# Output-projection pieces as separate jobs in the TensorE order table, and the last layer's norm on VectorE in another order

## Chip, cores and metric

One NeuronCore of one Trainium2 chip runs the whole program in one launch. Its engines work in parallel, each on its own in-order queue: TensorE (PE; matmuls, with PEld for its weight loads), VectorE (DVE), ScalarE (ACT), GpSimd (POOL), and SyncE (SP), which only starts DMAs here. The metric is the device time in microseconds (us), and less is better. Times are medians of several runs. One further execution was profiled, and all rows below are of that one.

## Reference

The kernel computes a trunk of four decoder layers on one sequence of 512 tokens with 1024 features. Layers 0 and 3 use latent attention (`mla`), layer 1 sliding-window attention (`swa`), layer 2 forgetting attention (`fox`). What matters here is the end of a layer:

```python
return (o * jax.nn.silu(gate)) @ w_out          # end of each branch
...
x = _layernorm(DEEPNORM_ALPHA * x + y, ln_g[i], ln_b[i])

def _layernorm(x, g, b):
    xf = x.astype(jnp.float32)
    mu = jnp.mean(xf, axis=-1, keepdims=True)
    var = jnp.mean(jnp.square(xf - mu), axis=-1, keepdims=True)
    y = (xf - mu) * lax.rsqrt(var + LN_EPS) * g.astype(jnp.float32) + b.astype(jnp.float32)
    return y.astype(x.dtype)
```

`o` holds 16 heads of width 64 side by side, so the output projection contracts over 1024 values: eight pairs of heads, 128 values each.

## The kernel before

**Tiling.** The 512 tokens are four blocks of 128 (`tb` 0 to 3). Matrix products are made of values split into a high and a low part, so a product of one 128-deep slice takes three matmuls: high x high, low x high and high x low (`tokproj_steps`; the order of the three is high-high, low-high, high-low for the left operand and the weight). A matmul writes up to 128 x 512 values into a PSUM bank. The pools of banks are `ps_p` (three banks, "pp" in the profile), `ps_s` and `ps_t` (two each) and `ps_o` (one, "oo").

**A layer.** Projections make the queries, keys, values and gates, pair by pair of heads. For each head there are logits (`s` steps; "ss"), a softmax on VectorE, ScalarE and GpSimd, transposes of the probabilities on TensorE (`t` steps; "ptt", evacuated by ScalarE at L500 and VectorE at L325 into "PT"), and the product with the values (`o` steps, `attn_pv`; "oo"). After the odd head of a pair, `attn_pv` evacuates the bank (ScalarE L543, VectorE L544), multiplies by the gate (GpSimd L551, VectorE for the last pair) and writes the pair's high part (ScalarE L552) and low part (L325) into the tile `oT`. These are the left operands of the output projection, so a matmul of the projection for pair k can run only when pair k is there.

**The output projection** gives 4 token blocks x 2 halves of 512 columns, each a sum over 8 pairs: 24 matmuls for one (half, block). `out_part` makes them in pieces: half 0 of blocks 0, 1 and 2 for the pairs 0 to 5 (18 matmuls each), then pair 6 of the same three (3 each), then half 1 of blocks 0, 1, 2 and half 0 of block 3 for the pairs 0 to 6 (21 each). Pair 7 is added at the end (`ends`, letter `k`), and half 1 of block 3 (`last_mm`, letter `m`) is made there as a whole. `out_part` is one generator, which gives these 147 matmuls in this fixed order.

**The order of TensorE** within a layer is written out by hand in the strings of `ORDER`. A word is a letter and a count: `s`, `t` and `o` are the steps named above; `f`, `g` and `h` take a step (in this part one matmul) of the first, second or third job of a list of unfinished jobs. The jobs are the projections of `STREAM`, and last of all the output projection as one job with 1000 steps. Where fewer jobs are left than the letter asks for, the index is cut to the last one:

```python
job = jobs[min("fgh".index(w[0]), len(jobs) - 1)] if w[0] in "fgh" else [0, runs[w[0]]]
```

So where the output projection alone is left, `f`, `g` and `h` all mean its next matmul. `tail` then adds the last two heads with fixed numbers of projection steps between them, and `finish` the end of the layer. During `ORDER` and `tail` only TensorE's order is as written; the other engines' orders are laid out when the program is built. In `finish` only VectorE's order is as written.

**The end of a layer** is the string of `FINISH` for that layer. Each word puts operations on VectorE and hands out the work for other engines that belongs to it:

- `f`, `k`, `m`: matmuls of the projection, as above.
- `r`, `h`, `i` (`out_res`, L586): residual plus projection for both halves, half 0 or half 1 of a block, in place in the tile `r`, with the row sums.
- `s` (`ln_stats`, L612 and L614): the negative mean on VectorE, then the squares of the whole block on ScalarE, added up.
- `t` (`ln_rstd`, L619 and L620): variance plus epsilon on VectorE, then the power -0.5 on GpSimd.
- `a` and `b` (`ln_apply`, L634): (r + negative mean) x gain, then x 1/sigma + offset; each is two passes of 128 x 512 on VectorE. `b` starts the DMA that stores the block. In the last layer block 3 goes to another tile (`y`) and is stored by halves.
- `z` (`ln_apply_side`, L645 to L651; last layer, block 0 alone): the same norm on ScalarE (one pass) and GpSimd (four passes).
- `x`: transposes of the block for the next layer (not in the last).

Of the kernel before, what the change touches and what calls it, by code (L numbers as in the profile page):

```python
# [12 lines left out]
F32 = mybir.dt.float32  # L13
F32R = mybir.dt.float32r
BF16 = mybir.dt.bfloat16
AF = mybir.ActivationFunctionType
ALU = mybir.AluOpType
# [3 lines left out]
D = 1024  # L21
S = 512
NT = S // 128
# [15 lines left out]
FINISH = (  # L39
# [4 lines left out]
)  # L44
PRO = ((2, 1, 2, 2), (2, 1, 19, 0))
TAIL = ((3, 4, 6, 6), (2, 10, 2, 5), (9, 0, 4, 9), (6, 3, 7, 2))
# [154 lines left out]
class Net:  # L201
# [355 lines left out]
    def out_part(self, layer, st):  # L557

        st["acc"] = {}
        st["done"] = 0  # L560
        st["stat"] = self.p_st.tile([128, NT, 4], F32, tag="stat", name=self.nm("stat"))
        self.load_residual(layer, st)
        parts = [(0, tb, range(6)) for tb in range(3)] + [(0, tb, [6]) for tb in range(3)]
        parts += [(half, tb, range(7)) for half, tb in ((1, 0), (1, 1), (1, 2), (0, 3))]
        for half, tb, ks in parts:
            for _ in self.out_mm(layer, st, half, tb, list(ks), False):
                st["done"] += 1 if self.fine else 3
                yield

    def out_mm(self, layer, st, half, tb, ks, stop):  # L570
        if (half, tb) not in st["acc"]:
            if (half, tb) in ((1, 0), (1, 1)):
                st["acc"][(half, tb)] = self.ps_s.tile([128, 512], F32, tag="ss", name=self.nm("po"))
            elif (half, tb) in ((1, 2), (0, 3)):
                st["acc"][(half, tb)] = self.ps_t.tile([128, 512], F32, tag="pt", name=self.nm("po"))
            else:
                st["acc"][(half, tb)] = self.bank()
        out = st["acc"][(half, tb)][:]
        oT = st["oT"]
        return self.tokproj_steps(out, lambda k: (self.W(layer, "O", half, k // 2), (k % 2) * 512), 512,  # L580
                                  lambda k, a, b: oT[k // 2][:, k % 2, a, b * 128:(b + 1) * 128], tb, ks, ks[0] == 0, stop, 3)
# [26 lines left out]
    def ln_stats(self, st, tb):  # L608
# [4 lines left out]
        jk = self.p_g.tile([128, D], BF16, tag="g", name=self.nm("jk"))  # L613
        nc.scalar.activation(jk[:], st["r"][tb][:], AF.Square, bias=s[:, 2:3], scale=1.0, accum_out=s[:, 3:4])  # L614

    def ln_rstd(self, st, tb):
        nc = self.nc
        s = st["stat"][:, tb, 3:4]
        nc.vector.tensor_scalar(s, s, 1.0 / D, LN_EPS, op0=ALU.mult, op1=ALU.add)  # L619
        nc.gpsimd.tensor_tensor(s, s, self.half[:, 0:1], op=ALU.pow)  # L620

    def ln_apply(self, layer, st, tb, part):
# [14 lines left out]
                nc.sync.dma_start(dst[:, cols], r[:, cols])  # L637
        if part and not halves:
            nc.sync.dma_start(dst, r[:])

    def ln_apply_side(self, st, tb):

        nc = self.nc
        r, s = st["r"][tb], st["stat"][:, tb]
        nc.vector.tensor_tensor(s[:, 2:3], s[:, 2:3], s[:, 3:4], op=ALU.mult)  # L645
        nc.scalar.activation(r[:], r[:], AF.Identity, bias=s[:, 2:3], scale=s[:, 3:4])
        for part, op in ((0, ALU.mult), (1, ALU.add)):
            for c in range(2):
                v = r[:, c * 512:(c + 1) * 512]
                nc.gpsimd.tensor_tensor(v, v, st["gb"][2 * part + c][:], op=op)  # L650
        nc.sync.dma_start(self.t["out"][tb * 128:(tb + 1) * 128, :], r[:])  # L651


    def run_heads(self, layer, st, make, pre=None, npre=0):

        kind = layer % 3
        st["P"], st["PT"], st["oT"] = {}, {}, []
        st["np"] = 3 if kind == 0 else 2
        self.heads = 0

        def size(n):
            return {"K": 6, "Q": 9, "R": 9}.get(n, 24) if kind == 0 else 96 if n == "V" else 24

        def logits():
            for h in range(H - 1):
                if h == 13 and kind == 0:
                    self.cq_done(layer)
                for i, f in enumerate(st["s_fn"](h, st)):
                    for j, _ in enumerate(f()):
                        if i == NT - 1 and j == st["np"] - 1:  # L670
                            self.head_done()
                        yield

        jobs = [[npre, pre]] if npre else []
        jobs += [[size(n), make[n](a)] for n, a in STREAM[kind]]
        st["order"] = self.out_part(layer, st)
        jobs.append([1000, st["order"]])
        runs = {"s": logits(), "t": chain.from_iterable(f() for h in range(H - 2) for f in st["t_fn"](h, st)),
                "o": chain.from_iterable(self.attn_pv(h, st) for h in range(H - 2))}
        self.fine = True  # L680
        with self.tc.manual_schedule(engines={mybir.EngineType.PE}):
            for w in ORDER[layer].split():
                for _ in range(int(w[1:])):
                    job = jobs[min("fgh".index(w[0]), len(jobs) - 1)] if w[0] in "fgh" else [0, runs[w[0]]]
                    next(job[1])
                    job[0] -= 1
                    while jobs[0][0] == 0:
                        jobs.pop(0)
            assert len(jobs) == 1 and all(next(r, None) is None for r in runs.values())
            self.tail(layer, st)  # L690

    def tail(self, layer, st):
# [12 lines left out]
    def finish(self, layer, st):  # L705
        nc = self.nc
        self.load_gb(layer, st)
        self.layer = layer + 1
        if layer < DEPTH - 1:
            self.new_xT()  # L710

        def mm(half, tb, ks=(7,)):
            self.run(self.out_mm(layer, st, half, tb, list(ks), True))

        def res(tb, half):
            self.out_res(layer, st, half, tb, st["acc"][(half, tb)][:])

        S0, S1 = lambda tb: self.ln_stats(st, tb), lambda tb: self.ln_rstd(st, tb)
        A = lambda tb, i: self.ln_apply(layer, st, tb, i)

        def X(tb):
            self.x_transposes(st["r"][tb], tb, (self.ps_s, "ss") if tb % 2 == 0 else (self.ps_t, "pt"))

        def ends(tb):
            assert st["done"] >= (84, 105, 126, 147)[tb]
            mm(0, tb)
            if tb < 3:
                mm(1, tb)

        last_mm = self.out_mm(layer, st, 1, 3, list(range(8)), True)  # L730
        todo = {"f": lambda n: self.run(islice(st["order"], n)), "k": ends, "m": lambda n: self.run(islice(last_mm, n)),
                "r": lambda t: (res(t, 0), res(t, 1)), "h": lambda t: res(t, 0), "i": lambda t: res(t, 1), "s": S0, "t": S1,
                "a": lambda t: A(t, 0), "b": lambda t: A(t, 1), "z": lambda t: self.ln_apply_side(st, t), "x": X}
        with self.tc.manual_schedule(engines={mybir.EngineType.DVE}):
            for w in FINISH[layer].split():
                todo[w[0]](int(w[1:]))
# [404 lines left out]
```

## Time and profile before

| | |
|---|---|
| median of 3 runs | 1026.9 us (1026.78 to 1029.99) |
| the profiled execution's own time | 1026.01 us |
| its span, first to last instruction | 1024.2 us |
| mean granted TensorE clock | 0.986 of full |
| DMA over the span | 116.79 MB, mean 114 GB/s |

How to read the rows: a timeline row has the start and the duration in us, the engine, the line of the program, the operation, output and inputs, the shape, and how many instructions were merged into it; in brackets stands the idle time of the engine before it and the instruction that ended it. L322 is the helper that issues every matmul, so matmuls are told apart by their tiles: "pp" or "po" with `oT` is the output projection. A wait row has the total, the number and the longest. A window row has the stretch, its length, the busy time of each engine with its number of instructions, the granted clock (1.00 is full), the share of DMA time and GB/s.

### The profile page before, as it was taken

The page shows a single profiled execution, that of the slowest core. Times are in us where ns is not written, and L with a number is a line of the kernel's source. Part 1 is how long each engine was busy: PE and PEld are TensorE (multiplying, and loading weights), DVE is VectorE, ACT ScalarE, POOL GpSimd, SP SyncE. Part 2 cuts the span into 40 slices and gives each one's busy share as a digit, 9 for nine tenths or more (in the row PEclk, how much of TensorE's full clock was granted, in tenths as well). Part 3 has the DMA queues.
Part 4 walks back from the last instruction along what each step waited for, and adds up shares of the span by engine and source line. Part 5 has one row for each costly group of instructions (what it writes and reads, how often), then busy time and mean ns, then how long its engine had stood idle before and what let it go on. Part 6 is the DMA issues. An engine that isn't in the chain of part 4 may idle for free.

```text
span 1024.2 us, 16213 instructions
## 1 busy us (share of the span) xinstructions
PE 985.8 (96%) x5512; PEld 856.9 (84%) x5512; DVE 598.3 (58%) x1501; ACT 620.8 (61%) x1354; POOL 510.7 (50%) x572
## 2 busy tenths in 40 slices
PE   8999999999999999899999999997999999999995
PEld 7979888877988888688888888985779888888784
DVE  2467666935546667528325644664547466667827
ACT  4378888843357777523446766663533478888722
POOL 5746655335156663432556666543254647664213
PEclk9999999999999999899999999998999999999998
DMA  6353332634342213223434323353224354334322
GB/s 225 119 157 92 98 106 66 205 111 146 133 143 84 83 63 124 91 94 128 133 120 141 105 88 120 91 144 120 84 84 146 97 145 127 85 94 124 103 62 83
DMA packets 37795, 116.79 MB, mean 114 GB/s; under 512 B 5440, under 2 KB 5696, under 8 KB 37456
## 3 DMA queue, kind: packets, MB, share of 16 engines
q1 hardware_dynamic: 37712, 115.75, 36.5%
q8 instruction: 44, 0.72, 0.3%
q14 instruction: 39, 0.32, 0.1%
HBM read 92.62 MB, written 8.42 MB: 99 GB/s over the span
## 4 chain that ended last, share of the span: by engine, by line
PE 47%; DVE 3%; issue 2%; POOL 1%; ACT 1%; DMA 1%; DVEq 0%; POOLq 0%; SPq 0%; ACTq 0%
PE pp L322 31%; PE ss L322 4%; PE po L322 4%; PE oo L322 3%; PE ptt L514 3%; DMA wr<-in_w 1%; PE pxt L389 1%; POOL r L650 1%; DVE w L310 1%; DVE r L634 0%; POOL P L462 0%; DVE PT L325 0%; ACT P L451 0%; DVE wo L310 0%; DVE r L586 0%
## 5 line engine op out<-in xcount | busy, mean ns | idle before, releaser
L322 PE MATMUL pp<-xT,w 128*128 128x512 f32 (+1 forms) x1440 | 352.4, 387 | 0.0
L310 POOL TENSOR_TENSOR w<-wr,w 128x512 fp32r<-128x512 f32 (+1 forms) x202 | 242.2, 1224 | 193.0 <-ACT w L306 127.2
L322 PEld LDWEIGHTS pp<-xT,w 128*128 128x128 f32 x1440 | 256.1, 188 | 44.2
L462 POOL TENSOR_TENSOR P<-P,rs 128x256 f32<-128x256 f32 (+2 forms) x192 | 113.0, 616 | 136.8 <-DVE rs L457 131.3
L306 ACT CAST w<-wr 128x1024 fp32r<-128x1024 f32 (+5 forms) x121 | 116.1, 964 | 87.4 <-PE pp L322 43.5
L451 ACT ACTIVATE P<-P,m 128x256 f32<-128x256 f32 (+3 forms) x256 | 137.8, 539 | 45.9 <-DVE m L1069 17.0
L325 DVE TENSOR_TENSOR PT<-ptt,PT 128x384 fp32r<-128x384 f32 (+1 forms) x176 | 104.0, 600 | 52.6 <-ACT PT L500 51.3
L500 ACT CAST PT<-ptt 128x384 fp32r<-128x384 f32 (+1 forms) x176 | 88.3, 515 | 47.6 <-PE ptt L514 34.6
L322 PE MATMUL pp<-w,xT 128*128 128x256 f32 (+2 forms) x768 | 112.7, 300 | 2.9 <-ACT xT L393 2.5
L322 PEld LDWEIGHTS pp<-w,xT 128*128 128x128 f32 x768 | 105.8, 191 | 4.6 <-ACT xT L393 3.1
L322 PE MATMUL oo<-PT,v 128*128 128x256 f32 (+3 forms) x512 | 106.6, 313 | 2.3 <-DVE o L544 1.6
L322 PEld LDWEIGHTS oo<-PT,v 128*128 128x128 f32 x512 | 83.5, 189 | 14.0 <-DVE o L544 2.6
L322 PE MATMUL pp<-w,oT 128*128 128x512 f32 x288 | 82.5, 422 | 10.9 <-ACT oT L552 7.5
L322 PE MATMUL ss<-kt,q 128*128 128x128 f32 (+3 forms) x384 | 81.8, 328 | 2.2 <-ACT kt L838 1.6
L322 PE MATMUL pp<-cT,w 128*128 128x512 f32 x312 | 81.6, 397 | 0.0
L885 DVE CUSTOM_DVE_ANT_0 P<-ss,mask 128x128 f32<-128x128 f32 (+3 forms) x128 | 61.1, 484 | 32.4 <-PE ss L322 24.7
L514 PE MATMUL ptt<-ident,P 128*128 128x128 f32 x480 | 78.5, 275 | 1.5 <-DVE PT L325 0.8
L322 PEld LDWEIGHTS pp<-w,oT 128*128 128x128 f32 x288 | 56.0, 202 | 23.4 <-ACT oT L552 8.1
L322 PE MATMUL po<-wo,oT 128*128 128x512 f32 x288 | 71.5, 396 | 0.0
L322 PEld LDWEIGHTS ss<-kt,q 128*128 128x128 f32 x384 | 60.7, 189 | 8.8 <-ACT kt L838 2.2
L514 PEld LDWEIGHTS ptt<-ident,P 128*128 128x128 f32 x480 | 57.1, 140 | 11.8 <-PE ss L322 2.1
L544 DVE TENSOR_TENSOR o<-oo,o 64x512 f32<-64x512 f32 x64 | 43.9, 686 | 37.4 <-ACT o L543 36.7
(120 smaller groups left out, 1425.9 us busy)
## 6 DMA issues: line engine op xcount, KB each, us to landing
wr<-in_w SPq DMA_DIRECT2D x106, 512.0 KB, 3.5
q<-rq SPq DMA_DIRECT2D x64, 128.0 KB, 2.4
xd<-r SPq DMA_DIRECT2D x12, 512.0 KB, 2.9
r<-xd SPq DMA_DIRECT2D x12, 512.0 KB, 3.4
wr<-in_w SPq DMA_DIRECT2D x16, 336.0 KB, 3.4
kd<-kd SPq DMA_DIRECT2D x20, 256.0 KB, 3.2
tq<-in_cs SPq DMA_DIRECT2D x8, 512.0 KB, 4.0
cb<-cd SPq DMA_DIRECT2D x16, 256.0 KB, 3.9
```

What stands on the lines that cost most here:

```text
L306: nc.scalar.copy(w[0][:, :c], r[:, :c])
L310: eng.tensor_tensor(w[1][:, a:b], r[:, a:b], w[0][:, a:b].bitcast(F32), op=ALU.subtract)
L322: self.nc.tensor.matmul(out, l, r, start=start, stop=stop)
L325: (eng or self.nc.vector).tensor_tensor(out, src, hi.bitcast(F32), op=ALU.subtract)
L389: nc.tensor.transpose(v, xt[:, c:c + 128], self.ident[:])
L451: nc.scalar.activation(v, v, AF.Exp, bias=m[:, c:c + 1], scale=-1.0, accum_out=sums[:, c:c + 1])
L462: nc.gpsimd.tensor_tensor(v, v, rs[:, c:c + 1].to_broadcast([128, v.shape[1]]), op=ALU.mult)
L500: nc.scalar.copy(pt[:, 0, :n], ps[:, :n])
L514: nc.tensor.transpose(ps[:, c:c + 128], Ps[qb][:, kb * 128:(kb + 1) * 128], self.ident[:])
L544: nc.vector.tensor_tensor(o[a, :], o_ps[a, :], o[a, :], op=ALU.add)
L650: nc.gpsimd.tensor_tensor(v, v, st["gb"][2 * part + c][:], op=op)
L885: nc.vector.tensor_tensor_reduce(out=P[:, :n], in0=ps[:, :n], in1=self.mask[:, S - n:], scale=1.0, scalar=3e38, op0=ALU.add, op1=ALU.min, ...
```

## The change

It has three parts. First, `out_part` no longer is one generator but returns a list of ten jobs, one for each piece, with its number of matmuls; they are appended to the list of jobs, and the index is not cut. So `g` and `h` now mean the next and the one after the next piece once only pieces are left. What is unfinished is chained for `tail`. The strings of `ORDER` are unchanged. Second, the last layer's string of `FINISH` has another order, and block 0's norm is made by `a0` and `b0` on VectorE; `ln_apply_side` is gone. Third, block 3's squares are made by halves (`p3`: the first half about its own mean, after `h3`; `q3`: the second half about the whole mean, after `i3`, with three small operations that correct the first half to the whole mean), and `t3` adds both.

```diff
-    'f14 k0 k1 k2 f99 r0 r1 s0 s1 t0 m1 z0 k3 r2 t1 s2 a1 m5 b1 m2 t2 h3 a2 b2 i3 s3 a3 t3 b3',
+    'f14 k0 k1 k2 f99 r0 r1 m1 k3 m7 s0 s1 a0 t0 r2 s2 t1 a1 b0 t2 b1 h3 p3 a2 b2 i3 q3 a3 t3 b3',
...
-        self.load_residual(layer, st)
         parts = [(0, tb, range(6)) for tb in range(3)] + [(0, tb, [6]) for tb in range(3)]
         parts += [(half, tb, range(7)) for half, tb in ((1, 0), (1, 1), (1, 2), (0, 3))]
-        for half, tb, ks in parts:
+
+        def part(half, tb, ks):
+            if "r" not in st:
+                self.load_residual(layer, st)
             for _ in self.out_mm(layer, st, half, tb, list(ks), False):
                 st["done"] += 1 if self.fine else 3
                 yield
+
+        return [[3 * len(ks), part(half, tb, ks)] for half, tb, ks in parts]
...
+    def ln_half(self, st, tb):
+        nc = self.nc
+        e, s = st["half"], st["stat"][:, tb]
+        nc.vector.tensor_scalar(e[:, 0:1], s[:, 0:1], -2.0 / D, None, op0=ALU.mult)
+        jk = self.p_g.tile([128, D // 2], BF16, tag="g", name=self.nm("jk"))
+        nc.scalar.activation(jk[:], st["r"][tb][:, :D // 2], AF.Square, bias=e[:, 0:1], scale=1.0, accum_out=e[:, 1:2])
+
+    def ln_other_half(self, st, tb):
+        nc = self.nc
+        e, s = st["half"], st["stat"][:, tb]
+        nc.vector.tensor_scalar(s[:, 2:3], s[:, 0:1], s[:, 1:2], -1.0 / D, op0=ALU.add, op1=ALU.mult)
+        jk = self.p_g.tile([128, D // 2], BF16, tag="g", name=self.nm("jk"))
+        nc.scalar.activation(jk[:], st["r"][tb][:, D // 2:], AF.Square, bias=s[:, 2:3], scale=1.0, accum_out=e[:, 2:3])
+        nc.vector.tensor_tensor(e[:, 3:4], s[:, 2:3], e[:, 0:1], op=ALU.subtract)
+        nc.vector.tensor_scalar(e[:, 3:4], e[:, 3:4], e[:, 3:4], D / 2.0, op0=ALU.mult, op1=ALU.mult)
+        nc.vector.tensor_tensor(e[:, 3:4], e[:, 3:4], e[:, 1:2], op=ALU.add)
...
     def ln_rstd(self, st, tb):
         nc = self.nc
         s = st["stat"][:, tb, 3:4]
+        if st.get("halves") == tb:
+            e = st["half"]
+            nc.vector.tensor_tensor(s, e[:, 3:4], e[:, 2:3], op=ALU.add)
...
-    def ln_apply_side(self, st, tb):
...
-        st["order"] = self.out_part(layer, st)
-        jobs.append([1000, st["order"]])
+        jobs += self.out_part(layer, st)
...
-                    job = jobs[min("fgh".index(w[0]), len(jobs) - 1)] if w[0] in "fgh" else [0, runs[w[0]]]
+                    job = jobs["fgh".index(w[0])] if w[0] in "fgh" else [0, runs[w[0]]]
...
-            assert len(jobs) == 1 and all(next(r, None) is None for r in runs.values())
+            assert all(next(r, None) is None for r in runs.values())
+            st["order"] = chain.from_iterable(g for _, g in jobs)
...
+        if "p3" in FINISH[layer]:
+            st["halves"] = NT - 1
+            st["half"] = self.p_st.tile([128, 4], F32, tag="half", name=self.nm("half"))
```

More of the change, by code (lines that the diff above doesn't have):

```diff
@@ L639, in ln_apply @@
             nc.sync.dma_start(dst, r[:])
-    def ln_apply_side(self, st, tb):
[L643 to L651, printed above, removed]
     def run_heads(self, layer, st, make, pre=None, npre=0):
@@ L732, in finish @@
                 "r": lambda t: (res(t, 0), res(t, 1)), "h": lambda t: res(t, 0), "i": lambda t: res(t, 1), "s": S0, "t": S1,
-                "a": lambda t: A(t, 0), "b": lambda t: A(t, 1), "z": lambda t: self.ln_apply_side(st, t), "x": X}
+                "a": lambda t: A(t, 0), "b": lambda t: A(t, 1), "p": lambda t: self.ln_half(st, t), "q": lambda t: self.ln_other_half(st, t), "x": X}
+        if "p3" in FINISH[layer]:
+            st["halves"] = NT - 1
+            st["half"] = self.p_st.tile([128, 4], F32, tag="half", name=self.nm("half"))
         with self.tc.manual_schedule(engines={mybir.EngineType.DVE}):
```

## The prediction

> **What bounds the kernel now.** I read the page first, then TensorE's waits, then the timeline around each long wait, then the windows of 2 us for the clock.
>
> ```profile
> span 1024.2 us, 16213 instructions
> PE 985.8 (96%) x5512; PEld 856.9 (84%) x5512; DVE 598.3 (58%) x1501; ACT 620.8 (61%) x1354; POOL 510.7 (50%) x572
> PEclk9999999999999999899999999998999999999998
> ```
>
> TensorE sets the time: 96% busy. Its granted clock, in 40 slices of 25.6 us, dips in slice 17 (410 to 435 us), in slice 28 (691 to 717 us) and in the last. So I ask what TensorE waits for; the columns are total us, times, longest.
>
> ```profile
> PE pp L322 <- ACT oT L552: 7.5, 2, 3.9
> PE pxt L389 <- DVE r L634: 4.4, 5, 2.0
> PE pp L322 <- POOL oT L325: 3.2, 2, 2.6
> ```
>
> The first and third rows are matmuls of the output projection that wait for the gated head outputs `oT`. The two waits on L552 are in layers 1 and 2. Timeline of layer 1 (start us, duration; in brackets the idle time before and its releaser), then windows of 2 us (PE busy, PEld, DVE, ACT, POOL, granted clock, DMA share, GB/s):
>
> ```profile
> 407.01 3.56 PE L322 MATMUL pp<-w,oT 128*128 128x512 f32 x15
> 410.42 0.40 PE L322 MATMUL ss<-kd,q 128*128 128x256 f32 x2
> 414.41 0.80 PE L322 MATMUL pp<-w,oT 128*128 128x512 f32 x1 [3.60 <-ACT oT L552]
> 415.76 5.96 PE L322 MATMUL pp<-w,oT 128*128 128x512 f32 x14
> 421.55 0.52 PE L322 MATMUL oo<-PT,v 128*128 128x256 f32 x3
> 425.33 1.05 PE L322 MATMUL oo<-PT,v 128*128 128x256 f32 x8
> ```
>
> ```profile
> 412.00:414.00 2.00, 0.00 (x0) 0.00 (x0) 1.97 (x4) 1.14 (x2) 1.28 (x1) 1.00 0.67 197
> 416.00:418.00 2.00, 2.00 (x5) 1.57 (x6) 0.33 (x3) 1.60 (x7) 0.00 (x0) 0.50 0.00 0
> 420.00:422.00 2.00, 2.00 (x9) 1.62 (x9) 0.00 (x0) 0.00 (x0) 0.68 (x2) 0.72 0.00 0
> ```
>
> Fifteen matmuls (output block 0, pairs 0 to 4) run at full clock; the sixteenth needs pair 5, and TensorE stands still 3.60 us. Then the clock is 0.50 until about 421 us: 14 matmuls take 5.96 us, where 15 took 3.56. So a wait costs twice. The same in layer 2:
>
> ```profile
> 705.24 0.80 PE L322 MATMUL pp<-w,oT 128*128 128x512 f32 x1 [3.90 <-ACT oT L552]
> 708.67 5.91 PE L322 MATMUL pp<-w,oT 128*128 128x512 f32 x13 [2.63 <-POOL oT L325]
> 714.39 0.53 PE L322 MATMUL oo<-PT,v 128*128 128x512 f32 x1
> ```
>
> ```profile
> 706.00:708.00 2.00, 0.04 (x1) 0.00 (x0) 0.00 (x0) 0.00 (x0) 2.00 (x3) 0.50 0.00 0
> 712.00:714.00 2.00, 2.00 (x7) 1.52 (x6) 0.00 (x0) 0.00 (x0) 0.00 (x0) 0.50 0.00 0
> ```
>
> **The order table, part by part.** Before, all output pieces are one job, so where only it is left `g` and `h` mean `f`. After, `g` is the next piece. Walking the four strings with the job sizes gives the same order in layer 0, and 6, 12 and 4 matmuls changed in layers 1, 2 and 3. No matmul is added or removed.
>
> Layer 1, from the two logit matmuls at 410.42 on. Before: block 0 pair 5 (with two logit matmuls inside), then block 1 pairs 0 to 3, then the three `oo`. After: block 1 pairs 0 to 4 (15 matmuls with the same two inside), the three `oo`, transposes, five `oo`, and only then the first matmul of block 0 pair 5. Layer 2 likewise: after, 14 matmuls of block 1 fill the place in front of the `oo`, and pair 5 comes later still.
>
> Price of one matmul at full clock, with the page's row of the same form (busy us, mean ns of one):
>
> ```profile
> L322 PE MATMUL po<-wo,oT 128*128 128x512 f32 x288 | 71.5, 396 | 0.0
> ```
>
> They overlap: the row at 407.01 holds 15 in 3.56 us; with the 0.40 us that a single one lasts taken off, 3.16/14 = 0.226 us from start to start. The two logit matmuls take 0.40 with their tail, 0.25 without.
>
> Layer 1: 3.60 us idle go. From 414.41 to 421.55 are 7.14 us for 15 matmuls and 2 logit ones; at full clock 15 x 0.226 + 0.25 = 3.6, so 3.5 go. Together 7.1. What is late next? `oT` of pair 5 first:
>
> ```profile
> 411.65 0.69 DVE L544 TENSOR_TENSOR o<-oo,o 64x512 f32<-64x512 f32 x1
> 413.45 0.68 DVE L410 SCALAR_TENSOR_TENSOR g<-g,pp 128x512 f32<-128x512 f32 x1
> 413.74 0.62 ACT L552 CAST oT<-o 128x512 fp32r<-128x512 f32 x1 [0.20 <-POOL o L551]
> 414.43 1.27 POOL L325 TENSOR_TENSOR oT<-o,oT 128x512 fp32r<-128x512 f32 x1 [0.73 <-ACT oT L552]
> 416.40 0.41 ACT L451 ACTIVATE P<-P,m 128x128 f32<-128x128 f32 x1 [2.05 <-DVE m L449]
> ```
>
> Its high part (the cast) is there at 414.4, its low part at 415.7. The new order asks for it after 15 matmuls and the `oo` and transposes, about 416.2: no wait. Then ScalarE: head 14's exponentials, today from 416.40 on (four passes with their reads, some 2.2 us as an estimate from that row), can start about 1 us sooner and then meet three evacuations (about 0.6 us each, as the cast at 413.74) on which the eight `oo` of 425.33 depend; these move forward to 418.2. If all three stand behind the exponentials, the eight are about 2.4 us late; if none, 0. I take 0.9, since both kinds become ready in turn. Layer 1: 6.2, bounds 4.7 and 7.3.
>
> Layer 2: 3.90 us idle go; from 705.24 to 714.39 are 9.15 us for 14 matmuls, against 14 x 0.226 = 3.2: 6.0 more, 9.9 in all.
>
> ```profile
> 702.43 0.69 DVE L544 TENSOR_TENSOR o<-oo,o 64x512 f32<-64x512 f32 x1
> 704.59 0.60 ACT L552 CAST oT<-o 128x512 fp32r<-128x512 f32 x1
> 707.36 1.26 POOL L325 TENSOR_TENSOR oT<-o,oT 128x512 fp32r<-128x512 f32 x1
> ```
>
> The new order asks for the high part about 706.2 (there at 705.2) and the low part about 710 (there at 708.6). VectorE and ScalarE are idle through 708 to 714 (window rows), so what follows can move forward with TensorE. I take off 0.3 for small waits: 9.6, bounds 7.5 and 9.9.
>
> Layer 3: four matmuls of the same kind change places. The two rows of waits on `oT` are 3.60, 3.90, 2.63 and one of 0.6, none of the long ones there: 0, bounds -0.6 and 0.6. Making each piece its own generator adds no instruction; the residual loads are still issued at the first piece.
>
> **The last layer's end.** After the eight matmuls of the last piece TensorE is done; VectorE decides the rest:
>
> ```profile
> 1002.81 1.15 ACT L614 ACTIVATE jk<-r,stat 128x1024 bf16<-128x1024 f32 x1 [10.64 <-DVE stat L612]
> 1008.60 5.01 PE L322 MATMUL pp<-wo,oT 128*128 128x512 f32 x21
> 1006.46 2.44 DVE L634 SCALAR_TENSOR_TENSOR r<-r,stat,P 128x512 f32<-128x512 f32 x2
> 1006.97 3.09 POOL L650 TENSOR_TENSOR r<-r,P 128x512 f32<-128x512 f32 x2
> 1016.56 0.67 DVE L586 SCALAR_TENSOR_TENSOR r<-r,pp 128x512 f32<-128x512 f32 x1
> 1017.28 0.21 DVE L612 TENSOR_SCALAR stat<-stat 128x1 f32<-128x1 f32 x1
> 1017.52 1.15 ACT L614 ACTIVATE jk<-r,stat 128x1024 bf16<-128x1024 f32 x1 [9.70 <-DVE stat L612]
> 1018.86 0.15 DVE L619 TENSOR_SCALAR stat<-stat 128x1 f32<-128x1 f32 x1
> 1019.66 1.41 DVE L634 SCALAR_TENSOR_TENSOR y<-y,stat,ln_b 128x512 f32<-128x512 f32 x2 [0.66 <-POOL stat L620]
> ```
>
> TensorE ends at 1013.6, but the last sum with the residual starts only at 1016.56. A pair of VectorE passes takes 1.41 us alone and 2.44 beside GpSimd's passes over block 0. The change takes block 0's passes from ScalarE and GpSimd and adds two pairs (2 x 1.41 us) to VectorE; all pairs should then take 1.41. The new list in order: the first pair (`a0`) overwrites what ScalarE's first square reads, so it starts only when that square is done, at 1004.1 (two squares of 1.15 us start at 1002.8); behind it in VectorE's queue stands `r2`, whose matmuls are long done. From 1004.1: `a0` 1.41, `t0` 0.15, `r2` 1.34, `s2` 0.21, `t1` 0.15, `a1` and `b0` 2.82, `t2` 0.15, `b1` 1.41, `h3` 0.67, `p3` 0.15, `a2` and `b2` 2.82: 1015.4. `i3` then needs nothing more from TensorE: 0.74, to 1016.1. `q3` puts four operations of one column on VectorE (0.21 + 3 x 0.15), `a3` 1.41: 1018.2. ScalarE's half square starts at 1016.35 (0.24 after its bias, as at 1017.28 to 1017.52) and lasts about half of 1.15 and a read: done by 1017.1, so VectorE and not ScalarE decides. `t3` now has two operations of 0.15, then the 0.80 us from 1018.86 to 1019.66: `b3` starts at 1019.1, 0.55 us before today's. The halved square by itself earns nothing, because `a3` covers it. GpSimd keeps the powers (three before the last, each shorter than the 0.66 us of waiting in the last row); if each stretches the pair beside it by its own length, 2.0 us are lost and the end is 1.5 later than today. If a pair is 2 x 0.67 long, as two residual sums, 0.5 more are won. I take 0.5, by the rows of the pairs that stood alone; bounds -1.5 and 1.1.
>
> **Sum**, on the profiled execution's 1026.0 us (span 1024.2 and 1.8 around it): 6.2 + 9.6 + 0 + 0.5 = 16.3, so 1009.7. The median shown is 0.9 above that execution; I state 1010.0. By the bounds: 10.1 to 18.9 us of gain.
>
> [...] The half clock lasted until about 421 and until about 714, in window rows of 0.50 more than 5 us after work had begun again at 414.41 and 708.67. [...]
>
> **Rivals.** (1) *A bank wait or ScalarE takes the place of layer 1's wait.* Block 1 needs a PSUM bank at 411 instead of 416. If it gets the last gate's, read until 414.1 (row 413.45), TensorE idles 3.3 us and the clock halves again: layer 1 gives about 0 to 1, time 1015.5. Against: three banks go round, and block 1 follows two after that of the gate before the last. ScalarE's 2.4 us late gives 1011.5. Together 0.14. (2) *Layer 2 keeps a wait*: after the moved block the `oo` need the bank that VectorE frees (row 702.43). If that comes late, half of 9.6 stays: 1014.5. Against: it is freed at 703.1, the `oo` come at 704.6. 0.05. (3) *The clock*: after layer 2 the rows show 2.03 us of waiting and then half clock.
>
> ```profile
> 765.09 0.66 PE L389 MATMUL pxt<-ident,r 128*128 128x128 f32 x4 [2.03 <-DVE r L634]
> 766.00:768.00 2.00, 1.98 (x7) 1.79 (x8) 2.00 (x3) 1.09 (x3) 2.00 (x3) 0.50 0.78 175
> ```
>
> Shifted by 16 us, the same wait may meet another phase of whatever samples the work; the drop, of at least the 2 us of that row and 3 us as an estimate, then goes, 1.5 us won: 1008.5. Against: the same wait, in the same place, made it. 0.08. [...] (4) *The order table does not do what it says*, and only the end counts: 1025.5, 0.03. (5) *Slower*: only TensorE's and, at the end, VectorE's orders are written out; ScalarE's is made anew. If head 14's exponentials and gate work came ahead of pair 5's cast (L552) in both layers, TensorE would wait at the later place. It decides once the two new waits with their half clock cost more than the 16.3 us won; with casts 6 us late at each place and the half clock behind, some 9.5 us each, and 1.5 lost at the end, 1030. Against: ScalarE is busy 1.14 of 2 us there. 0.03. Forecast: 0.67.
>
> A measurement of this kernel tells about 0.3% (3 us) from no change. Faster: 0.67 + 0.14 + 0.05 + 0.08 = 0.94; same 0.03; slower 0.03. The range, 1006.0 to 1016.0, takes in the bounds of the sum and the rivals (1) to (3).
>
> **What would show it.** No wait of `pp` on `oT` above 1 us; clock 1.00 through 410 to 422 and at the corresponding place in layer 2; the last residual sum within 2.5 us of TensorE's end, with pairs of 1.4 us and no GpSimd pass beside them. Wrong if a new wait of over 3 us stands in layer 1 or 2, with half clock behind it, or if pairs stay above 2 us.

## The result, and the profile after

The changed kernel takes 1011.69 us (median of 4 runs, 1010.53 to 1012.74), the kernel before 1026.84 us in the same comparison (4 runs, 1026.27 to 1029.99). The ratio is 0.9846 with a 95% interval of 0.9822 to 0.987: 15 us or 1.5% faster. The profiled execution of the changed kernel took 1012.59 us with a span of 1010.8 us. The page and TensorE's longest waits:

```profile
span 1010.8 us, 16221 instructions
PE 981.7 (97%) x5512; PEld 854.6 (85%) x5512; DVE 599.2 (59%) x1509; ACT 620.0 (61%) x1355; POOL 505.4 (50%) x568
PEclk9999999999999999999999999999999999999999
```

```profile
PE oo L322 <- DVE o L544: 4.6, 4, 1.5
PE pxt L389 <- DVE r L660: 4.5, 4, 2.2
PE pp L322 <- ACT xT L393: 1.8, 1, 1.8
```

The waits of `pp` on `oT`, 7.5 and 3.2 us before, are gone, and so are the dips of the clock in the 40 slices. The row at the top has grown: `oo` waits for VectorE's evacuation (L544), 4 times, 4.6 us in all. Before, it was

```profile
PE oo L322 <- DVE o L544: 1.6, 3, 0.9
```

To see where the time went I cut both executions at five marks that every kernel has: (A) the 15 matmuls of output block 0 in layer 1, (B) the second group of transposes (`pxt`) at the end of layer 1, (C) the first group that waits at the end of layer 2, (D) the 21 last matmuls of the last piece, and (E) VectorE's last pair. Here are the marks after, and B of before (its other marks stand in the prediction):

```profile
408.43 3.56 PE L322 MATMUL pp<-w,oT 128*128 128x512 f32 x15
...
462.41 0.66 PE L389 MATMUL pxt<-ident,r 128*128 128x128 f32 x4 [1.02 <-DVE r L660]
...
752.48 0.66 PE L389 MATMUL pxt<-ident,r 128*128 128x128 f32 x4 [2.18 <-DVE r L660]
...
996.45 5.01 PE L322 MATMUL pp<-wo,oT 128*128 128x512 f32 x21
...
1006.23 1.42 DVE L660 SCALAR_TENSOR_TENSOR y<-y,stat,ln_b 128x512 f32<-128x512 f32 x2 [0.66 <-POOL stat L646]
```

```profile
465.73 0.66 PE L389 MATMUL pxt<-ident,r 128*128 128x128 f32 x4 [1.02 <-DVE r L634]
```

| stretch | before | after | difference | predicted |
|---|---|---|---|---|
| start to A (layer 0, most of layer 1) | 407.01 | 408.43 | +1.42 | 0 |
| A to B (end of layer 1) | 58.72 | 53.98 | -4.74 | -6.2 |
| B to C (layer 2) | 299.36 | 290.07 | -9.29 | -9.6 |
| C to D (layer 3) | 243.51 | 243.97 | +0.46 | 0 |
| D to E (the last norm) | 11.06 | 9.78 | -1.28 | -0.5 |

The columns add up to -13.43, the difference of the two spans (13.4).

**Layer 1.** The timeline around the place, with the rows of ScalarE and VectorE that matter:

```profile
412.53 3.37 PE L322 MATMUL pp<-w,oT 128*128 128x512 f32 x14
417.22 0.40 ACT L451 ACTIVATE P<-P,m 128x128 f32<-128x128 f32 x1 [1.42 <-DVE m L449]
417.58 2.10 PE L322 MATMUL pp<-w,oT 128*128 128x512 f32 x8
419.29 0.56 ACT L500 CAST PT<-ptt 128x512 fp32r<-128x512 f32 x1
419.87 0.58 ACT L543 COPY o<-oo 64x512 f32<-64x512 f32 x1
420.49 0.68 DVE L544 TENSOR_TENSOR o<-oo,o 64x512 f32<-64x512 f32 x1
421.23 0.62 PE L322 MATMUL oo<-PT,v 128*128 128x256 f32 x3 [1.54 <-DVE o L544]
422.01 0.79 PE L322 MATMUL oo<-PT,v 128*128 128x256 f32 x5 [0.17 <-DVE PT L325]
```

TensorE runs through at 412.53, where it stood still for 3.60 us before. But ScalarE makes all of head 14's exponentials (L451, from 417.22) ahead of the evacuations L500 and L543, and so the eight `oo` of head 13 come 1.54 and 0.17 us late. The rest of the matmuls between, the eight from 417.58, were done at 419.68.

**Layer 2.** The same place has no wait, and the clock stays full for 18 us (timeline, then one window):

```profile
697.78 4.13 PE L322 MATMUL pp<-w,oT 128*128 128x512 f32 x17
701.75 0.39 PE L322 MATMUL oo<-PT,v 128*128 128x512 f32 x1
```

```profile
700.00:718.00 18.00, 16.67 (x92) 13.57 (x91) 11.76 (x43) 13.11 (x34) 9.87 (x11) 1.00 0.26 88
```

**The end.** VectorE's and GpSimd's rows of the last layer after:

```profile
991.95 1.42 DVE L660 SCALAR_TENSOR_TENSOR r<-r,stat,P 128x512 f32<-128x512 f32 x2 [1.19 <-ACT jk L618]
994.87 1.41 DVE L660 SCALAR_TENSOR_TENSOR r<-r,stat,P 128x512 f32<-128x512 f32 x2
995.03 1.00 POOL L646 TENSOR_TENSOR stat<-stat,half 128x1 f32<-128x1 f32 x1 [0.96 <-DVE stat L645]
1002.34 0.68 DVE L590 SCALAR_TENSOR_TENSOR r<-r,pp 128x512 f32<-128x512 f32 x1
1003.38 0.72 ACT L634 ACTIVATE jk<-r,stat 128x512 bf16<-128x512 f32 x1 [2.69 <-DVE stat L632]
1003.91 1.41 DVE L660 SCALAR_TENSOR_TENSOR y<-r,stat,P 128x512 f32<-128x512 f32 x2
1005.23 0.15 DVE L644 TENSOR_TENSOR stat<-half 128x1 f32<-128x1 f32 x1
1005.65 0.55 POOL L646 TENSOR_TENSOR stat<-stat,half 128x1 f32<-128x1 f32 x1 [6.92 <-DVE stat L645]
```

All pairs of the last layer take 1.40 to 1.42 us now (2.41 to 3.48 before, where GpSimd's passes ran beside them). The last residual sum starts at 1002.34, 0.88 us after TensorE's end (996.45 + 5.01 = 1001.46); before it was 2.95. A power of GpSimd beside a pair is stretched itself (1.00 us at 995.03, 0.55 alone at 1005.65), and the pair is not.

### The profile page after: what moved, and what is told of

It reads as the page before. It is cut to its first block, busy times and chain, and to the rows that moved or that the text cites. A ratio compares the mean times of both kernels' runs of the same rounds, so it can differ in the third digit from the quotient of the medians.

```text
span 1010.8 us, 16221 instructions
## 1 busy us (share of the span) xinstructions
PE 981.7 (97%) x5512; PEld 854.6 (85%) x5512; DVE 599.2 (59%) x1509; ACT 620.0 (61%) x1355; POOL 505.4 (50%) x568
## 4 chain that ended last, share of the span: by engine, by line
PE 45%; DVE 3%; issue 3%; POOL 2%; ACT 1%; DMA 1%; DVEq 0%; POOLq 0%; SPq 0%; ACTq 0%
PE pp L322 30%; PE ss L322 4%; PE po L322 4%; PE oo L322 3%; PE ptt L514 3%; POOL w L310 1%; DVE r L660 1%; PE pxt L389 1%; DMA cb<-cd 0%; DVE PT L325 0%; DMA q<-rq 0%; ACT PT L500 0%; DVE r L590 0%; DVE wo L310 0%; PE pc L823 0%
## 5 line engine op out<-in xcount | busy, mean ns | idle before, releaser
L451 ACT ACTIVATE P<-P,m 128x256 f32<-128x256 f32 (+3 forms) x256 | 137.7, 539 | 45.1 <-DVE m L1086 17.3
L500 ACT CAST PT<-ptt 128x384 fp32r<-128x384 f32 (+1 forms) x176 | 88.4, 515 | 35.6 <-PE ptt L514 24.7
L322 PE MATMUL pp<-w,oT 128*128 128x512 f32 x288 | 76.1, 398 | 0.0
L544 DVE TENSOR_TENSOR o<-oo,o 64x512 f32<-64x512 f32 x64 | 43.9, 686 | 37.5 <-ACT o L543 36.7
L322 PEld LDWEIGHTS pp<-cT,w 128*128 128x128 f32 x312 | 56.6, 188 | 10.4
```

The costliest lines, as they stand in the source:

```text
L322: self.nc.tensor.matmul(out, l, r, start=start, stop=stop)
L451: nc.scalar.activation(v, v, AF.Exp, bias=m[:, c:c + 1], scale=-1.0, accum_out=sums[:, c:c + 1])
L500: nc.scalar.copy(pt[:, 0, :n], ps[:, :n])
L544: nc.vector.tensor_tensor(o[a, :], o_ps[a, :], o[a, :], op=ALU.add)
```

## The experiments

All stretches below are read from the profiled execution of each kernel at the marks A to E. This table is the result of all of them; medians and intervals stand with each experiment.

| kernel | start to A | A to B | B to C | C to D | D to E |
|---|---|---|---|---|---|
| before | 407.01 | 58.72 | 299.36 | 243.51 | 11.06 |
| the change | 408.43 | 53.98 | 290.07 | 243.97 | 9.78 |
| order table in all layers | 408.93 | 54.01 | 289.55 | 241.74 | 11.07 |
| order table, layer 1 | 407.44 | 53.86 | 299.42 | 243.11 | 11.07 |
| order table, layer 2 | 410.00 | 58.24 | 289.26 | 244.67 | 11.08 |
| last norm alone | 408.27 | 58.19 | 299.26 | 242.78 | 9.78 |
| squares whole | 409.53 | 53.81 | 289.32 | 243.72 | 8.82 |
| r2 first | 410.90 | 54.13 | 289.37 | 243.91 | 8.95 |
| cover in layer 1 | 410.91 | 55.38 | 289.51 | 243.55 | 9.77 |
| all three | 406.57 | 55.30 | 289.43 | 242.37 | 8.17 |
| both edits of the end | 409.98 | 53.89 | 289.31 | 242.98 | 8.17 |
| all, and a piece moved | 411.80 | 51.56 | 289.33 | 243.63 | 8.18 |

Where two kernels have the same code in a stretch, the stretch agrees within 0.8 us in layers 1 and 2 and within 0.02 us at the end. The first column, with the same layer 0 in all twelve, spreads over 5.2 us (five of the twelve executions had half clock near 211 us), and the fourth over 2.9. So the medians of some few runs tell parts of 1 us apart badly, and the stretches tell them apart well.

### The order table alone, in all layers and in one

The kernel before, with the pieces as jobs of their own in the layers that `PIECES` names: all, only layer 1, only layer 2.

```diff
+PIECES = (0, 1, 2, 3)
...
-        st["order"] = self.out_part(layer, st)
-        jobs.append([1000, st["order"]])
+        pieces = self.out_part(layer, st)
+        jobs += pieces if layer in PIECES else [[147, chain.from_iterable(g for _, g in pieces)]]
```

All layers:

> The order table as in the change, the last layer's end as before. Theory A (the gain is the two waits on the head outputs with their half clock): 14.0 to 15.0 us less than before, so about 1012.3. Rival B (the new end of the last layer brings several us, or depends on the order table): the gain is under 12 us.

Measured: 1013.54 us (4 runs, 1010.52 to 1017.93) against 1026.97 before, ratio 0.9866 [0.9821, 0.991]. These 13.4 us are a little under the 14.0 to 15.0 expected, within the interval.

Only layer 1:

> Only layer 1 takes each output piece as its own job; the other layers and the end as before. Theory A: the wait of 3.6 us and the half clock behind it go, and a wait of the eight products with the values on VectorE and ScalarE, 1.5 us with half clock behind it, comes: 4.7 us less than before, 1022.1. Rival B (layer 1's gain is given back later, in layer 2): within 1 us of before.

Measured: 1021.24 us (10 runs, 1018.79 to 1028.57), ratio 0.9949 [0.9925, 0.9973]. The wait expected on VectorE and ScalarE came (1.66 us), the half clock behind it did not in this execution; A to B is 4.86 us shorter than before, where 4.7 were expected.

Only layer 2:

> Only layer 2 takes each output piece as its own job. Theory A: 9.3 us less than before, 1017.5, with no wait of over 1 us in its place. [...]

Measured: 1019.62 us (7 runs, 1015.81 to 1021.92), ratio 0.9912 [0.9885, 0.9938]. The 7.4 us by the medians are 1.9 us under the 9.3 of theory A. The stretch B to C decides: 10.1 us less than before, and no wait above 0.46 us at the place of the old ones.

What follows: by the medians the single layers give 5.7 and 7.4 us, together 13.1, and the table in all layers 13.4. The medians alone could not show that the two gains add up; the stretches do, since each layer's is the same with and without the other's new order. Layer 1's, A to B, falls from 58.2 to 58.7 (three kernels with the old order) to 53.8 to 54.1 (six with the new one), 4.4 us. Layer 2's, B to C, falls from 299.3 to 299.4 to 289.3 to 290.1, 9.3 to 10.1 us. Layer 2 gives what the prediction put down for it and layer 1 gives less.

### The last norm alone

The changed kernel with the pieces put back together into one job.

```diff
-        jobs += self.out_part(layer, st)
+        jobs.append([147, chain.from_iterable(g for _, g in self.out_part(layer, st))])
...
-                    job = jobs["fgh".index(w[0])] if w[0] in "fgh" else [0, runs[w[0]]]
+                    job = jobs[min("fgh".index(w[0]), len(jobs) - 1)] if w[0] in "fgh" else [0, runs[w[0]]]
```

> Only the last layer's norm in its new order with the squares by halves; the order table as before. Theory A: 0.5 to 1.0 us less than before, 1026.1, which is within what a run can tell; in the trace, from the last weight of TensorE to the start of the last pair of VectorE passes 4.8 us instead of 6.1, no GpSimd pass beside VectorE's. Rival B: VectorE, which now has all the passes, is late: 1 us or more slower than before.

Measured: 1025.55 us (10 runs, 1023.66 to 1030.31), ratio 0.9993 [0.9972, 1.0014]: by the median no difference that can be told. The stretch D to E is 9.78, the same as in the change, against 11.06 to 11.08 in the four kernels with the old list: the end is worth 1.28 us, a size that only the trace shows. It is what was expected there: 4.77 us from TensorE's end to the last pair, where the kernel before has 6.05.

### The halves, and r2 ahead

First the changed kernel with block 3's squares whole; then with block 2's residual sums ahead of block 0's first pair.

```diff
-    'f14 k0 k1 k2 f99 r0 r1 m1 k3 m7 s0 s1 a0 t0 r2 s2 t1 a1 b0 t2 b1 h3 p3 a2 b2 i3 q3 a3 t3 b3',
+    'f14 k0 k1 k2 f99 r0 r1 m1 k3 m7 s0 s1 a0 t0 r2 s2 t1 a1 b0 t2 b1 h3 a2 b2 i3 s3 a3 t3 b3',
```

> The change with the last block's squares in one piece again (s3 in the place of p3 and q3). Measure in the trace: from TensorE's end to the start of the last pair of VectorE passes, 4.77 us in the changed kernel. Theory A: VectorE's own queue sets this, and the halves put four dependent small operations (0.84 us) in front of the pair a3, so whole squares make it 4.1 to 4.3. Rival B: ScalarE's squares set it, and whole squares make it about 5.2. In the time less than a run can tell either way: 1011.1 by A, 1012.1 by B.

Measured: 1011.57 us (4 runs, 1010.7 to 1012.67) against 1025.84, ratio 0.9853 [0.9833, 0.9874].

```diff
-    'f14 k0 k1 k2 f99 r0 r1 m1 k3 m7 s0 s1 a0 t0 r2 s2 t1 a1 b0 t2 b1 h3 p3 a2 b2 i3 q3 a3 t3 b3',
+    'f14 k0 k1 k2 f99 r0 r1 m1 k3 m7 s0 s1 r2 a0 t0 s2 t1 a1 b0 t2 b1 h3 p3 a2 b2 i3 q3 a3 t3 b3',
```

> The change with r2 ahead of a0 in VectorE's list, so that VectorE adds block 2's residual while ScalarE still reads block 0. Theory A: the 1.19 us that VectorE waits in front of a0 go, the last sum with the residual starts when TensorE ends, and the last pair starts 4.0 us after TensorE's end instead of 4.77. Rival B: the 1.19 us were idle time that costs nothing, 4.7 as before. In the time -0.8 by A, 0 by B.

Measured: 1010.78 us (4 runs, 1010.05 to 1013.61), ratio 0.9843 [0.9819, 0.9867].

What follows: neither median differs from the change's. The stretch D to E does: 9.78 in the change, 8.82 with whole squares, 8.95 with `r2` first. From TensorE's end to the last pair these are 4.77, 3.81 and 3.94 us, so theory A holds in both, and with whole squares the gain is larger than it said (4.1 to 4.3). The halves cost 0.96 us. The reason is in the end's rows above: ScalarE's half square (1003.38, 0.72 and a read) is done at 1004.2; a whole one of 1.15 would be done at 1004.7; either is over before the pair `a3` ends at 1005.3. So the squares were covered already; what the halves add stands on VectorE, ahead of `a3` (three small operations; `a3` starts 1.57 us after the start of the last residual sum, 0.97 where the squares are whole), ahead of the last power (L644), and once ahead of `i3`. With `r2` first VectorE works through ScalarE's first square, where it waited 1.19 us, and after that it is TensorE that is late:

```profile
1003.36 0.69 DVE L590 SCALAR_TENSOR_TENSOR r<-r,pp 128x512 f32<-128x512 f32 x1 [0.41 <-PE pp L322]
```

### Cover for layer 1's new wait

Six matmuls of the output projection more between head 13's two groups of `oo`, taken from those behind.

```diff
-TAIL = ((3, 4, 6, 6), (2, 10, 2, 5), (9, 0, 4, 9), (6, 3, 7, 2))
+TAIL = ((3, 4, 6, 6), (2, 8, 2, 5), (9, 0, 4, 9), (6, 3, 7, 2))
...
-    "f1 o1 f3 o2 f1 o5 t7 s4 f19 s2 f1 s2 f4 o1 f6 o7 t7 s2 f1 s2 f19 s2 g1 s2 g14 o3 t4 o5 f1 t3 g1 f7 o8",
+    "f1 o1 f3 o2 f1 o5 t7 s4 f19 s2 f1 s2 f4 o1 f6 o7 t7 s2 f1 s2 f19 s2 g1 s2 g14 o3 t4 o5 f1 t3 g1 f13 o8",
```

> The change with six matmuls of layer 1's output projection moved from behind the products of head 14 to the place in front of the eight products of head 13 that wait in the changed kernel. Theory A: the wait of 1.5 to 1.7 us on VectorE and ScalarE there goes, and with it the half clock that follows it in some executions; no new wait of over 0.5 us; 1.7 to 3.2 us less than the changed kernel, about 1009.5. Rival B: the softmax of head 14 or 15 is then late and TensorE waits for it instead: same as the changed kernel, 1011.7.

Measured: 1011.36 us (6 runs, 1008.78 to 1015.48), ratio 0.9855 [0.9831, 0.9879]. TensorE in its timeline:

```profile
423.76 0.61 PE L322 MATMUL oo<-PT,v 128*128 128x256 f32 x3 [0.21 <-DVE o L544]
...
432.81 3.25 PE L322 MATMUL pp<-w,oT 128*128 128x512 f32 x8 [1.96 <-POOL oT L325]
```

The wait for the evacuation shrinks from 1.54 to 0.21 us, as it should. A wait of 1.96 us for the low part of pair 6 takes its place, since the matmuls that stood ahead of pair 6 are used up sooner. Neither theory had this: the median is that of rival B, but no softmax was late. The four waits of this stretch ahead of its end add up to 2.58 us here and to 2.67 us in the kernel with the end's two edits below, which has layer 1 as in the change: the cover only moved the waiting. A to B becomes longer, 55.38 against 53.98: in layer 1 this edit loses 1.4 us. Behind the new wait the clock is halved while TensorE has work throughout:

```profile
433.46:436.88 3.42, 3.42 (x10) 2.64 (x9) 0.15 (x1) 0.13 (x1) 1.22 (x3) 0.50 0.59 206
```

All three edits together:

> The changes of the three other kernels of this call together: whole squares, r2 ahead of a0, six matmuls as a cover in layer 1. Theory A: 1.3 us less at the end and 1.7 to 3.2 less in layer 1: about 1008. Rival B: no better than the changed kernel, 1011 to 1012.

Measured: 1011.1 us (5 runs, 1008.22 to 1011.74), ratio 0.9839 [0.9818, 0.986]. By the median this is rival B. D to E is 8.17, 1.6 us less than in the change; A to B is 55.30, with the same wait for pair 6 and half clock behind it (429.72 to 433.14), so the end's part of theory A came and layer 1's did not.

### The end's two edits, and a piece moved in layer 1

Two kernels follow from this: one leaves layer 1 as the change has it, and one takes away what pair 6 makes TensorE wait for. The first:

```diff
-    'f14 k0 k1 k2 f99 r0 r1 m1 k3 m7 s0 s1 a0 t0 r2 s2 t1 a1 b0 t2 b1 h3 p3 a2 b2 i3 q3 a3 t3 b3',
+    'f14 k0 k1 k2 f99 r0 r1 m1 k3 m7 s0 s1 r2 a0 t0 s2 t1 a1 b0 t2 b1 h3 a2 b2 i3 s3 a3 t3 b3',
```

> The changed kernel with two edits of the last layer's list alone: block 3's squares whole, and block 2's residual sums ahead of block 0's first normalizing pass. Layers 0 to 2 as in the changed kernel. In the kernel with all three edits the stretch from TensorE's last matmul to the last pair's start was 3.16 us, in the changed kernel 4.77. Theory A (these two edits alone set that stretch, whatever layer 1 does): 3.1 to 3.2 us here, 1.6 us won, 1010.1 by the median of 1011.7. Theory B (part of the 1.6 us came from how TensorE's end lay against VectorE after the other layer 1): 3.8 us or more, 1011 or above. Executions differ by some us, so the stretch in the trace decides and not the median.

Measured: 1008.66 us (5 runs, 1007.72 to 1010.68) against 1025.51 before, ratio 0.9829 [0.9808, 0.9849]. The median is 1.4 us under the 1010.1 expected; the trace was to decide. The last matmul ends 3.16 us ahead of the last pair (996.16 + 5.01 to 1004.33), as in the kernel with all three edits: theory A. Layer 1 does not matter for it.

The second has this, the end's two edits and the cover:

```diff
         parts += [(half, tb, range(7)) for half, tb in ((1, 0), (1, 1), (1, 2), (0, 3))]
+        if layer == 1:
+            parts[3:7] = [(1, 0, range(6)), *parts[3:6], (1, 0, [6])]
```

> As the kernel with all three edits, and in layer 1 the piece (half 1, block 0, pairs 0 to 5) stands ahead of the three pieces of pair 6; its pair 6 follows as a piece of its own. Theory A (the wait of 1.96 us on the low part of pair 6 came because the six matmuls moved ahead let pair 6 be asked for earlier, and 18 matmuls, 4.1 us, cover it): no wait above 0.5 us in layer 1 from the output projection's first matmul on, no half clock there, so 1.96 us and a half-clock stretch worth 1.7 us less than with all three edits; about 1007.5 by its median of 1011.1. Theory B (pair 6 is late by more, through ScalarE's and GpSimd's queues, since TensorE now runs further ahead): a wait of 1 us or more on an oT or an oo comes at another place of layer 1, and the median stays within 1009.5 to 1012. Theory C (the bank of the moved piece is still held by the logits): a wait of a po on VectorE or ScalarE of 1 us or more.

Measured: 1009.6 us (4 runs, 1005.49 to 1010.85), ratio 0.9833 [0.9807, 0.9859]. TensorE in layer 1:

```profile
424.67 0.62 PE L322 MATMUL oo<-PT,v 128*128 128x256 f32 x3 [0.24 <-DVE o L544]
425.46 0.80 PE L322 MATMUL oo<-PT,v 128*128 128x256 f32 x5 [0.17 <-DVE PT L325]
...
430.63 0.90 PE L322 MATMUL pp<-w,oT 128*128 128x512 f32 x3
431.37 4.32 PE L322 MATMUL po<-wo,oT 128*128 128x512 f32 x18
435.54 0.86 PE L322 MATMUL pp<-w,oT 128*128 128x512 f32 x3
```

The moved piece (18 matmuls, 4.32 us) stands where TensorE waited; no wait in the stretch is above 0.24 us but the 1.02 at its end, which all kernels have. A to B is 51.56: 2.42 us less than in the change, and 7.16 less than before. That is close to the 7.1 us which the prediction put down as the whole of layer 1's loss, ahead of its deduction (against the two other kernels with the old order in layer 1 it is 6.6 and 6.7). From A to E this kernel is the shortest of all (592.70 us; 594.35 with the end's edits alone, 597.80 the change, 612.65 before). Its profiled execution lost that again in layer 0, which it has in common with the others (411.80 up to A). The expected median of 1007.5 was not reached, though the wait went as in theory A. The medians of these two kernels cannot be told apart. Both lie under the change's, by 3.0 and 2.1 us, but the ratios to the kernel before (0.9829 and 0.9833, and 0.9846 for the change) have intervals that overlap. So it is the stretches that show both to be better than the change, by 1.6 us at the end and 2.4 in layer 1, and the times do not contradict.

## Why the prediction was right, and where it was off

The direction and the range held, and of the 16.9 us predicted by the medians 15.2 came; 1010.0 is 1.7 us too low. From the profiled execution, 1009.7 was predicted and 1012.59 came. Of these 2.9 us layer 1 makes 1.5, layer 0, whose order is the same, 1.4, layers 2 and 3 make 0.3 and 0.5, and the end gave 0.8 more than predicted. The number stated does not quite follow from the sum either: the median of 1026.9 less 16.3 is 1010.6 and not 1010.0. That the 1.7 us look small is in part luck, since a term too large and a term too small offset each other. Step by step:

**Layer 1, the step that was mis-sized.** The wait for pair 5 went with its half clock, as predicted, and the gross 7.1 us were about right (6.6 to 7.2 measured with the new wait covered). The deduction failed: "If all three stand behind the exponentials, the eight are about 2.4 us late; if none, 0. I take 0.9, since both kinds become ready in turn." All of them stood behind the exponentials, and 2.42 us were lost, as the kernel with the moved piece shows. That this is the upper bound is in part coincidence: the eight themselves were 1.71 us late and not 2.4, and the rest of the loss is the half clock behind them or, where the clock stayed full, a wait of 0.60 us for pair 6, which is made from them. The place was read rightly from the rows; the choice between the bounds was not. What decides is in the rows of after. The first transposes that L500 evacuates were through at 416.69,

```profile
416.09 0.60 PE L986 MATMUL ptt<-ident,P 128*128 128x128 f32 x4
```

yet ScalarE stood idle until 417.22, when head 14's maximum (L449) released the exponentials, made all of them, and began L500 only at 419.29. What became ready in turn was not taken in turn here: the transposes were there 0.53 us before the exponentials could start, and their evacuation began 2.07 us after them, behind all four. (Whether anything else still held L500 at 416.69 the rows do not show; ScalarE's order was not changed in a run.) 4.74 is just inside the bounds (4.7 to 7.3). The prediction gave this case 0.14 together with another, as its first rival, at 1011.5; it is what happened, beside a better end.

**Layer 2.** 9.6 predicted, 9.29 measured, 9.8 to 10.1 in the eight other kernels with its new order. The 0.3 "for small waits" was hardly needed; the mechanism and the price were right. The walk through the strings was not read quite rightly: "6, 12 and 4 matmuls changed" is not the number that moves. By the strings 3, 5 and 2 matmuls move past others in layers 1, 2 and 3. No term of the sum goes by these counts.

**Layers 0 and 3.** The order in layer 0 is unchanged, yet A came 1.42 us later. The last group of `oo` of a head waits there in each kernel, 0.38 us before and 1.48 after:

```profile
202.83 1.05 ACT L306 CAST wo<-wr 128x1024 fp32r<-128x1024 f32 x1 [2.69 <-DMA wr<-in_w]
208.48 1.19 PE L322 MATMUL oo<-PT,v 128*128 128x512 f32 x5 [1.48 <-DVE o L544]
```

ScalarE waited 2.69 us for a weight DMA just ahead, 0.87 before. Among the twelve executions that wait goes from 0.38 to 2.67 us. I take it for a difference from run to run, since kernels with the old and the new order stand on both sides (1.50 with the last norm alone, 0.55 with layer 1's order table alone); what makes the DMA late was not tried. Layer 3 was predicted at 0 and gave +0.46, inside the spread of its column.

**The end.** 0.5 predicted, 1.28 measured. The pairs took 1.41 us and the powers did not stretch them, as taken. The list from the first pair to the last residual sum was mis-sized by 0.9 us: 11.3 us by adding the durations, 10.39 in the trace (991.95 to 1002.34), because an operation starts before the duration of the one ahead of it is over (a pair of 1.41 is followed after 1.33). "The halved square by itself earns nothing, because `a3` covers it" is right about the cover. It should have been read as a loss: the same list counted four small operations ahead of `a3`, and the runs put them at 0.8 to 1.0 us.

**How long the half clock lasted.** The prediction read it from windows of 2 us, as "more than 5 us after work had begun again". Stretches of 3.41 us, by which the half clock begins and ends in these traces (last section), show it more closely. Before, layer 1 and layer 2 (columns as in the prediction's windows):

```profile
410.89:414.31 3.42, 0.00 (x0) 0.00 (x0) 3.36 (x6) 1.76 (x3) 1.46 (x2) 1.00 0.72 229
414.31:417.72 3.41, 3.19 (x8) 2.41 (x9) 0.82 (x5) 1.36 (x7) 1.27 (x1) 0.50 0.00 0
417.72:421.13 3.41, 3.41 (x10) 2.63 (x9) 0.34 (x2) 1.35 (x6) 1.54 (x3) 0.50 0.00 0
421.13:424.54 3.41, 3.41 (x24) 3.07 (x23) 1.38 (x3) 1.65 (x3) 0.00 (x0) 1.00 0.02 5
...
704.44:707.85 3.41, 0.80 (x1) 0.29 (x1) 0.17 (x1) 0.75 (x2) 3.41 (x6) 0.50 0.07 25
707.85:711.27 3.42, 2.60 (x6) 2.11 (x7) 0.00 (x0) 0.00 (x0) 0.77 (x1) 0.50 0.00 0
711.27:714.68 3.41, 3.41 (x9) 2.64 (x9) 0.00 (x0) 0.00 (x0) 0.00 (x0) 0.50 0.00 0
```

The half clock lasts two such windows in layer 1 (to 421.13) and three in layer 2 (to 714.68), 6.7 and 6.0 us after work had begun again at 414.41 and 708.67, and ends with the first in which TensorE is busy throughout. The sum took the whole loss from the rows, and so holds.

**The third rival, the clock after layer 2.** The 3 us of the drop were the author's estimate; before, it lasted 3.41 us (765.88 to 769.29, clock 0.50). In the change it stayed (754.07 to 757.49). In two kernels with the same code there it did not come: the order table in all layers, and all three edits. Their C to D, 241.74 and 242.37, stands against 242.78 to 243.97 in the nine executions with this one drop: about 1.4 us, where the rival was priced at 1.5. It is a matter of the run and not of the change. The slower rival, ScalarE's work ahead of pair 5's cast, did not come.

## What to carry to other kernels

Where an order written out by hand takes away one wait, ask of every evacuation between there and the next wait what stands ahead of it in its engine's queue, and price it at the bound at which all of that comes first (here 2.42 us, where 0.9 was put down), unless the rows show that it is ready later. Before work is split to shorten a step, ask whether that step ends last: here another engine's pair covered it, and the extra small operations were the whole effect (0.96 us). For parts of 1 us compare stretches between marks of the trace, not medians.

## What the runs showed of the hardware

**Half clock comes on a grid.** In each execution all stretches of half clock begin and end on one grid of 3.413 us, from the start of the program to its end. Before, they begin at 8.12, 414.31, 704.44 and 765.88 us: 119, 85 and 18 such steps apart (406.19, 290.13, 61.44). In the next execution the grid lies elsewhere (9.97, 422.98, 754.07 after).

**How little idle time halves the clock.** After, and with the end's two edits, whose TensorE waits 1.69 and 0.17 us at the same place of layer 1, cut on the grid of each execution:

```profile
419.57:422.98 3.41, 1.70 (x12) 1.38 (x12) 2.03 (x5) 1.89 (x5) 1.54 (x3) 1.00 0.00 0
422.98:426.39 3.41, 3.41 (x16) 3.31 (x16) 2.91 (x11) 1.56 (x4) 1.52 (x2) 0.50 0.00 0
```

```profile
418.65:422.07 3.42, 2.59 (x14) 1.82 (x12) 1.07 (x4) 3.12 (x12) 0.62 (x3) 1.00 0.02 5
422.07:425.48 3.41, 2.38 (x18) 2.17 (x19) 1.96 (x6) 1.55 (x4) 1.14 (x2) 1.00 0.00 0
425.48:428.89 3.41, 3.20 (x21) 2.74 (x21) 3.35 (x11) 2.19 (x4) 2.48 (x2) 1.00 0.46 145
```

In the first the wait falls into one window, TensorE is busy 1.70 of 3.41 us, and the next window runs at half clock. In the second an edge cuts the wait in two, 2.59 and 2.38 us are busy, and nothing happens. In eleven traces (all but that of the cover in layer 1), up to the window in which TensorE ends, every window at full clock with 1.70 us or less busy was followed by half clock (28 windows), none with 2.13 or more was, and of the 13 between 5 were. One window at TensorE's end goes against this, and the clock stayed full for one window more (after):

```profile
999.83:1003.25 3.42, 1.63 (x8) 0.98 (x6) 3.38 (x7) 0.82 (x2) 0.00 (x0) 1.00 0.38 153
```

So the bounds are no sharper than this, also because busy times are modelled at their ends. A window at half clock in which TensorE was busy throughout (3.39 us or more) brought the full clock back each time; those with 3.1 to 3.3 us busy went both ways. Waits of 1.69, 2.08 and 2.09 us left the clock full in three of these traces, and waits of 1.54 and 2.03 us halved it in two others: where the grid falls is different in each execution.

**Half clock can be free.** A to B takes 53.98, 54.01 and 54.13 us in three executions with a window of half clock there, and 53.86, 53.89 and 53.81 in three without. Where TensorE is not slowed, it meets the low part of pair 6, which VectorE, ScalarE and GpSimd deliver in their own time (the kernel with the end's two edits):

```profile
432.01 2.11 PE L322 MATMUL pp<-w,oT 128*128 128x512 f32 x8 [0.60 <-POOL oT L325]
```

So the 2.42 us in layer 1 are lost with or without the half clock. It did cost time where TensorE had nothing to wait for: by the sums of waits above behind the wait for pair 6 in the kernels with the cover (1.4 us), and after layer 2, where the two executions without the drop were 1.4 us shorter.
